# A second float32 weight group issued from ScalarE's DMA queue instead of SyncE's

## The chip, the cores and the metric

One core of a Trainium2 chip. The metric is the device time of the kernel in microseconds (us); the median of several runs is given.

## The reference

```python
batch, dim_i, dim_j, dim_k = 32, 256, 256, 128      # all inputs float32

def reference(x, y, weight):
    return np.einsum('bi,bj,kij->bk', x, y, weight).astype(np.float32)
```

The weights are 128 x 256 x 256 x 4 bytes = 33.6 MB. x, y and the output are 32, 32 and 16 KB. So this is a kernel that streams weights.

## The kernel before

The weights are cut into 32 groups of 1.05 MB. In a group each of 128 partitions holds one row of 8 KB. The kernel multiplies in bf16, and there are two ways to get there:

- 30 groups are loaded by GpSimd's DMA queue, which casts on the way ("casting loads" below). They are 11 copies, taken in order.
- Groups 0 and 16 (`FIRST`) are loaded as float32 by SyncE's queue into `w_f`, and ScalarE casts them into `w_sb`. They exist because GpSimd's loads take some microseconds to start moving data (the first casting packet starts at 5.59 us here).

```python
LOADS = (
    ((8, 24), 0, 8),
    ((4, 12, 20, 28), 0, 8),
    (tuple(range(2, 32, 4)), 0, 8),
    # ... cut: eight more, down to eighths of the last group
)
FIRST = (0, 16)

    # ... cut: shapes, buffers, semaphores
    sw = [ nc.gpsimd.dma_start(out=w_of(groups)[...], in_=rows_of(groups)[...]).then_inc(s, 16).ins
           for (groups, lo, hi), s in zip(LOADS, s_w) ]                    # shortened
    hw = [
        nc.scalar.dma_start(out=x_sb, in_=x).then_inc(s_x, 16).ins,
    ]
    for n, g in enumerate(FIRST):
        hw.append(
            nc.sync.dma_start(
                out=w_f[:, n:n + 1, :], in_=rows_of((g,)),
            ).then_inc(s_f[n], 16).ins
        )
    # ... cut: these issues are moved to the very head of the program, before the start barrier

    for n, g in enumerate(FIRST):
        for h in range(2):
            lo, hi = h * IC * J // 2, (h + 1) * IC * J // 2
            c = act.copy(out=w_sb[:, place_of[g], lo:hi], in_=w_f[:, n, lo:hi])
            if h == 0:
                c._wait_ge(s_f[n], 16)
            c.then_inc(s_act, 1)

    # ... cut: VectorE prepares xblk and y4
    pe.wait_ge(s_act, 2 * len(FIRST))
    pe.wait_ge(s_dve, t_x)
    # ... cut: TensorE multiplies unit by unit, waiting for each load; the first unit of
    #     16 groups holds groups 0 and 16 and needs the first three casting loads too
```

## Time and profile before

| | before |
|---|---|
| median of 3 runs | 84.71 us |
| span in the profile | 83.4 us |
| DMA engines working | about 1.2 to 80.8 us |
| first matmul | 41.93 us |
| TensorE / VectorE / ScalarE busy | 39% / 30% / 6% of the span |

A profile's slices tell when an engine works, but a busy engine is not yet the bound. What counts is which wait ends last: here TensorE, between its last units, stands and waits for weights. The prediction below shows those lines. To them belong the DMA queues of the kernel before (queue and kind, packets, MB, share of the 16 engines' span): q1 is SyncE's, q10 is ScalarE's.

```profile
q1 hardware_dynamic: 432, 2.11, 6.8%
q10 hardware_dynamic: 48, 0.03, 0.1%
```

SyncE's queue carries both float32 groups, ScalarE's only x. The page counts both queues' packets as a share of the same 16 DMA engines, and the trace has 16 completion entries (packets of 4 bytes) for each copy of either: 48 for SyncE's three copies, the output among them, and 16 for x.

Where a text below counts single packets ("started at", "packets of 8 KB"), the numbers come from the packet records of the trace. A copy of one float32 group is 128 packets of 8 KB, 8 for each DMA engine. A casting packet writes 4 KB of bf16 (3712 such packets in the trace), for which 8 KB of float32 are read. The records don't say which engine ran a packet, so "for each engine" is a count divided by 16, and a "round" is 16 packets.

### The profile page before, as it was taken

To read this page: it belongs to the slowest core of one execution; us is meant where nothing else is said; L and a number is where in the kernel's file an instruction comes from. 1 tells how busy PE (TensorE), PEld (TensorE's weight loads), DVE (VectorE), ACT (ScalarE), POOL (GpSimd) and SP (SyncE) were. 2 spreads that over 40 slices of the span, in tenths; PEclk is the share of its full clock that TensorE was granted. 3 is DMA by queue.
4 is the path that set the end of the run, shared out by engine and by line. 5 is a ranking of instruction groups with operands and counts; after the bars stand their busy time and mean duration, and the time that the engine had idled before them with its cause. 6 is when DMAs were issued, how large, how long until landed. Compare 5 with 4: busy or idle time off the path is not lost.

```text
span 83.4 us, 257 instructions
## 1 busy us (share of the span) xinstructions
PE 32.6 (39%) x136; PEld 4.3 (5%) x43; DVE 25.1 (30%) x28; ACT 5.2 (6%) x5; POOL 8.8 (11%) x18
## 2 busy tenths in 40 slices
PE   0000000000000000000089999996019999984780
PEld 0000000000000000000000000000000100112330
DVE  0009450000292000000000000003999900999932
ACT  0019930000000000000000000000000000000000
POOL 5999600000000000000000000000000000000000
PEclk9999999999999999999999999999995699999999
DMA  4999999999999999999999999999999999999980
GB/s 126 373 377 301 218 208 216 216 214 216 218 218 210 218 216 210 216 218 212 216 216 210 216 218 212 216 216 210 218 216 212 216 216 210 216 218 210 200 115 8
DMA packets 4912, 17.91 MB, mean 215 GB/s; under 512 B 384, under 2 KB 800, under 8 KB 4656
## 3 DMA queue, kind: packets, MB, share of 16 engines
q0 software_dynamic: 4432, 15.76, 94.3%
q1 hardware_dynamic: 432, 2.11, 6.8%
q10 hardware_dynamic: 48, 0.03, 0.1%
HBM read 33.62 MB, written 0.02 MB: 403 GB/s over the span
## 4 chain that ended last, share of the span: by engine, by line
DMA 46%; PE 39%; DVE 6%; POOL 3%; another core or an unknown queue 3%; issue 2%; POOLq 0%
DMA w_sb<-in_weight_dram 46%; PE ps L237 39%; DVE tmp L294 5%; POOL w_sb L120 2%; POOL y_sb L127 1%; DVE tmp L302 1%; POOL const-float32-0.0 L332 0%; POOLq L332 0%; POOL const-uint8-127 L332 0%; POOL const-float32-1.0 L332 0%; DVE acc L302 0%
## 5 line engine op out<-in xcount | busy, mean ns | idle before, releaser
L237 PE MATMUL ps<-w_sb,xblk 128*128 128x512 bf16 (+1 forms) x136 | 32.6, 397 | 48.9 <-DMA w_sb<-in_weight_dram 44.2
L294 DVE TENSOR_TENSOR tmp<-ps,y 128x4096 f32<-128x4096 f32 (+3 forms) x4 | 8.6, 2156 | 36.7 <-PE ps L237 36.7
L298 DVE TENSOR_REDUCE acc<-tmp 128x16 f32<-128x4096 f32 (+3 forms) x4 | 8.6, 2155 | 0.1
L237 PEld LDWEIGHTS ps<-w_sb,xblk 128*128 128x128 bf16 x43 | 4.3, 101 | 77.0 <-DMA w_sb<-in_weight_dram 42.7
L120 POOL DMA_DIRECT2D w_sb<-in_weight_dram x11 | 7.6, 702 | 0.6 <-issue 0.6
L178 ACT CAST w_sb<-w_f 128x1024 bf16<-128x1024 f32 x4 | 3.9, 1041 | 0.0
L219 DVE STREAM_TRANSPOSE yt<-y_sb 32x256 f32<-32x256 f32 x1 | 0.4, 433 | 11.0 <-DMA y_sb<-in_y_dram 11.0
L192 DVE COPY x_rep<-x_sb 32x1024 f32<-32x1024 f32 x1 | 0.8, 786 | 6.1 <-PEq L332 6.1
L198 DVE STREAM_TRANSPOSE xt<-x_rep 32x256 f32<-32x256 f32 x4 | 1.7, 435 | 0.1
L227 DVE STREAM_TRANSPOSE y<-y_rep 32x256 f32<-32x256 f32 x4 | 1.7, 435 | 0.1
L178 ACT ACT_TABLE_LOAD x1 | 1.3, 1283 | 6.0 <-PEq L332 6.0
L210 DVE TENSOR_SCALAR xblk<-xt,mask 128x256 bf16<-128x256 f32 x4 | 1.4, 498 | 0.0
L302 DVE CUSTOM_DVE_ANT_0 tmp<-ps,y 128x256 f32<-128x256 f32 x2 | 0.8, 425 | 1.6 <-PE ps L237 1.6
L222 DVE COPY y_rep<-yt 32x1024 f32<-32x1024 f32 x1 | 0.7, 683 | 0.0
L205 DVE TENSOR_REDUCE mask<-ident 128x4 f32<-128x128 f32 x1 | 0.4, 382 | 1.0 <-POOL ident L169 1.0
L127 POOL DMA_DIRECT2D y_sb<-in_y_dram x1 | 0.5, 534 | 0.0
L169 POOL TENSOR_SCALAR_AFFINE_SELECT ident<-ident 128x128 f32<-128x128 f32 x1 | 0.3, 287 | 0.1
L168 POOL MEMSET ident<- 128x128 f32 x1 | 0.3, 289 | 0.0
L302 DVE DVE_READ_ACCUMULATOR2_ANT acc<- 128x1 f32 x2 | 0.2, 84 | 0.0
L332 POOL MEMSET const-float32-0.0<- 128x1 f32 x1 | 0.1, 98 | 0.2 <-issue 0.2
L332 POOL MEMSET const-bfloat16-1.0<- 128x1 bf16 x1 | 0.1, 101 | 0.0
L332 POOL MEMSET const-uint8-127<- 128x1 uint8 x1 | 0.1, 101 | 0.0
(1 smaller groups left out, 0.1 us busy)
## 6 DMA issues: line engine op xcount, KB each, us to landing
w_sb<-in_weight_dram POOLq DMA_DIRECT2D x2, 4096.0 KB, 48.0
w_sb<-in_weight_dram POOLq DMA_DIRECT2D x2, 2048.0 KB, 43.3
w_f<-in_weight_dram SPq DMA_DIRECT2D x2, 1024.0 KB, 6.6
w_sb<-in_weight_dram POOLq DMA_DIRECT2D x2, 1024.0 KB, 40.9
w_sb<-in_weight_dram POOLq DMA_DIRECT2D x1, 512.0 KB, 72.2
w_sb<-in_weight_dram POOLq DMA_DIRECT2D x1, 256.0 KB, 72.8
w_sb<-in_weight_dram POOLq DMA_DIRECT2D x1, 128.0 KB, 72.9
w_sb<-in_weight_dram POOLq DMA_DIRECT2D x2, 64.0 KB, 72.7
```

The lines of the kernel that those rows point to most:

```text
L120: nc.gpsimd.dma_start(out=w_of(groups)[:, :, lo * J:hi * J], in_=rows_of(groups)[:, :, lo * J:hi * J],).then_inc(s, 16).ins
L127: sw.insert(2, nc.gpsimd.dma_start(out=y_sb, in_=y).then_inc(s_y, 16).ins)
L178: c = act.copy(out=w_sb[:, place_of[g], lo:hi], in_=w_f[:, n, lo:hi])
L192: t = done(v.tensor_copy(out=x_rep, in_=x_sb.rearrange("b (ip ic) -> b ic ip", ic=IC).unsqueeze(3) .to_broadcast([B, IC, IP, KK]),)._wait_ ...
L198: c = v.transpose(out=xt[q * 32:(q + 1) * 32, :, :], in_=x_rep[:, :, q * IP // Q:(q + 1) * IP // Q, :],)
L210: c = v.tensor_scalar(out=xblk[:, :, :, kk], in0=xt, scalar1=mask[:, kk:kk + 1], scalar2=None, op0=mult,)
L222: t = done(v.tensor_copy(out=y_rep, in_=yt.unsqueeze(3).to_broadcast([B, J // 32, B, KK]),)._wait_ge(s_dve, t))
L227: c = v.transpose(out=y4[q * 32:(q + 1) * 32, :].rearrange("p (jb j) -> p jb j", j=32), in_=y_rep[:, :, q * BQ:(q + 1) * BQ, :],)
L237: return pe.add_instruction(mybir.InstMatmult(name=nc.get_next_instruction_name(), engine=mybir.EngineType.PE, ins=[pe.lower_ap(rhs), pe.l ...
L294: t = done(v.tensor_tensor(out=prod, in0=sums, in1=y4.unsqueeze(1).to_broadcast([P, n_g, J]), op=mult,)._wait_ge(s_pe, n_pe))
L298: done(v.tensor_reduce(out=acc[:, unit[0]:unit[-1] + 1:unit[1] - unit[0]], in_=prod, axis=AX, op=add,)._wait_ge(s_dve, t))
L302: done(v.tensor_tensor_reduce(out=prod[:, 0, :], in0=sums[:, 0, :], in1=y4, scale=1.0, scalar=0.0, op0=mult, op1=add, accum_out=acc[:, uni ...
```

## The change

The intent: SyncE's second issue waits behind its first (0.61 us each). ScalarE has only issued x by then, so it can issue the second group at the same time, on a queue of its own.

```diff
-    for n, g in enumerate(FIRST):
+    for n, (g, queue) in enumerate(zip(FIRST, (nc.sync, nc.scalar))):
         hw.append(
-            nc.sync.dma_start(
+            queue.dma_start(
                 out=w_f[:, n:n + 1, :], in_=rows_of((g,)),
             ).then_inc(s_f[n], 16).ins
         )
```

## The prediction

Where "row" isn't a row of weights or of a profile, in the prediction and in the texts below, it means the DMA queue of an issuing engine.

> **What bounds the kernel now.** I read the page first. Its slices show where work is missing, its chain shows which work the end waits for.
>
> The slices (40 of 2.085 us; mean busy tenths of the 16 DMA engines, then GB/s counted as written), and the chain's shares of the span:
>
> ```profile
> DMA  4999999999999999999999999999999999999980
> GB/s 126 373 377 301 218 208 216 216 214 216 218 218 210 218 216 210 216 218 212 216 216 210 216 218 212 216 216 210 218 216 212 216 216 210 216 218 210 200 115 8
> ...
> DMA 46%; PE 39%; DVE 6%; POOL 3%; another core or an unknown queue 3%; issue 2%; POOLq 0%
> ```
>
> The DMA engines are full from the second slice to the second last. The chain gives PE 39% and so looks split, but it follows PE only because matmuls happen to be running; the chain in order of time shows that PE is fed group by group and goes back to waiting for weights.
>
> ```profile
> 3.17 38.71 DMA w_sb<-in_weight_dram
> ...
> 76.16 1.89 PE ps L237 x8
> 78.04 0.49 another core or an unknown queue
> 78.53 0.04 issue
> 78.57 1.03 PE ps L237 x8
> ```
>
> After each of the late units (here 1.89 us of matmuls) there is idle time that an arriving transfer ends; the page's group of the matmuls names it (48.9 us idle, 44.2 of it for weights). So the end is set by the last weight bytes, plus a tail of 2 to 3 us. The metric is some 84.7 us, of which the DMA stream takes about 1.2 to 80.8.
>
> What the stream carries, in stretches (columns: stretch, length, busy us of the five engines, clock, DMA share, GB/s written):
>
> ```profile
> 1.00:1.25 0.25, 0.00 (x0) 0.00 (x0) 0.00 (x0) 0.00 (x0) 0.20 (x1) 1.00 0.20 57
> 1.25:1.50 0.25, 0.00 (x0) 0.00 (x0) 0.00 (x0) 0.00 (x0) 0.25 (x1) 1.00 1.14 369
> 1.50:2.00 0.50, 0.00 (x0) 0.00 (x0) 0.00 (x0) 0.00 (x0) 0.50 (x2) 1.00 0.91 246
> 2.00:2.50 0.50, 0.00 (x0) 0.00 (x0) 0.00 (x0) 0.00 (x0) 0.50 (x1) 1.00 0.93 262
> 2.50:5.50 3.00, 0.00 (x0) 0.00 (x0) 0.00 (x0) 0.00 (x0) 3.00 (x5) 1.00 1.02 410
> 5.50:6.50 1.00, 0.00 (x0) 0.00 (x0) 0.42 (x1) 0.46 (x1) 1.00 (x3) 1.00 1.01 315
> 6.50:8.00 1.50, 0.00 (x0) 0.00 (x0) 1.40 (x4) 1.49 (x2) 1.50 (x3) 1.00 1.05 319
> 8.00:12.00 4.00, 0.00 (x0) 0.00 (x0) 2.45 (x7) 3.22 (x4) 1.64 (x5) 1.00 1.06 213
> 12.00:70.00 58.00, 23.49 (x93) 1.62 (x15) 11.70 (x8) 0.00 (x0) 0.00 (x0) 0.97 1.06 215
> ```
>
> A GpSimd-issued weight load reads 4 bytes for each 2 that it writes, so 215 GB/s written is 430 read. A float32 copy writes what it reads: 410 is 410. The two kinds thus differ in this column, and it tells which is running: up to 5.5 us only float32; from 5.5 to 8.0 a mixture (half of 410 and half of 213 would be 311; seen 315 and 319); after 8.0 the casting loads alone. Between 2.5 and 70 us the reading rate is 410 to 430, with no gap. Only 1.25 to 2.5 us is short of it.
>
> [...]
>
> **The change part by part.** Issues and their use, in the timeline, and the landings of the two groups, in the view of their tile:
>
> ```profile
> 0.00 1.26 SPq L134 DMA_DIRECT2D w_f<-in_weight_dram  x2
> 0.12 0.41 ACTq L130 DMA_DIRECT2D x_sb<-in_x_dram  x1
> ...
> 6.04 1.28 ACT L178 ACT_TABLE_LOAD   x1 [6.04 <-PEq L332]
> ...
> 7.33 3.88 ACT L178 CAST w_sb<-w_f 128x1024 bf16<-128x1024 f32 x4
> ```
>
> ```profile
> L134 SPq DMA_DIRECT2D w_f<-in_weight_dram x2: 586/606/627, 0.0 to 0.7; - x2
> ...
> DMA to landing us min/median/max: 4.9/6.6/8.2
> ```
>
> 1. Issue. SyncE loses one issue of about 0.61 us and ScalarE gains it. Second group now: starts about 0.65, ends 1.26. After: behind x, 0.12 + 0.41 + 0.61 = 1.14. That is 0.12 us earlier, and it is saved on no path, since the first group keeps the DMA engines in work well past that. SyncE next has the output at 82 us. ScalarE waits for a start signal until 6.04 us, so its extra 0.61 us lies in 5.5 us of idle time. Cost 0.
> 2. Bytes. The same 2 x 1.05 MB of float32, the same 31.5 MB read by casting loads, the same 16 engines. Change 0.
> 3. Landings. Up to 5.5 us the stretches sum to 14 + 92 + 123 + 131 + 1230 = 1590 KB, of which 33 are x, so 1.56 of 2.10 MB of float32 are through. Now these are the whole first group and half of the second. Afterwards the second group's first bytes should come some 0.8 us after its issue ended, as the first group's do (issue over at 0.6, first bytes about 1.4): 1.95 us. Until then the first has a lead of some 0.16 MB; then they alternate. At 5.5 us: 0.86 and 0.70 MB. With three rows active each reads a third of 430, 143 GB/s: first group through after (1.05 - 0.86)/0.143 = 1.3 us, at 6.8; the second then has 0.16 MB left at 215, through at 7.6. Landing follows the last bytes by about 0.65 us (8.2 to 8.9 now). So I expect **7.5 and 8.2 us from the span's start, against 4.9 and 8.9 now**.
> 4. Casts. The first starts at 7.33 now, when the table is loaded; it would start near 7.5. Casts end near 11.4 instead of 11.21. The first matmul is at 41.93, held by the third casting load. Slack 30 us; cost 0.
> 5. Casting loads. They give up a sixth of the rate from 5.5 to 6.8 us and have the engines alone from 7.6 instead of about 8.2. This cancels, as bytes are the same.
> 6. Start-up. Short of 430 GB/s are 1.25 to 2.5 us by 538 - 346 = 192 KB and 2.5 to 5.5 us by 60 KB: together 0.59 us at 430 GB/s, all that better feeding could win. The second row has data only from about 1.95, so it can fill 0.55 x (430 - 262) = 92 KB and the 60 KB: 152 KB, 0.35 us. The profile doesn't tell whether the shortage belongs to one row (then gained) or to the first reads whatever the row (then not). I give it somewhat less than half: 0.15 us.
>
> Sum: 84.71 - 0.15 = 84.56, rounded to 84.6.
>
> **The rivals.**
> - *The second row ends the slow start.* For it: DMA share 0.91 to 0.93 there against 1.05 later, at 60% of the rate, so packets are open but slow. Against: the slow time is nearly over when the second row gets data. It makes 84.3.
> - *Interleaved groups disturb each other in HBM* (the 4 MiB pitch). [...] Against: the casting loads of groups 8 and 24 (also 4 MiB apart) and the mixture at 5.5 to 8.0 run at full rate[...]. [...] I hold it for improbable[...].
> - *ScalarE becomes late* and with it the casts. Its slack of 30 us speaks against it; it makes no change.
> - *The casting loads start later*, because three rows share instead of two, or *earlier*. Only work-conserving reshuffling while the DMA row stays full; 84.7.
>
> **Range and chances.** Before's runs spread 84.64 to 84.9. The full start-up gain gives 84.36, none 84.71, slight disturbance 84.9; with the spread: 84.25 to 84.95. To be over 2% faster takes 1.7 us, almost three times all the shortage there is: 0.01. To be over 2% slower takes the HBM rival at full size: 0.02. Within 2%: 0.97.
>
> **What would show it.** Right: slices full of DMA as before; landings near 7.5 and 8.2; the mixture ends near 7.6 and its written rate is higher in its first part (two thirds float32: about 350 GB/s); first matmul at 41.9 within 0.4 us, all later unit waits shifted by the same amount. The start-up term is read in the stretches 1.5 to 5.5 us: 262 and 410 higher is the gain. Wrong: a float32 stretch under 380 GB/s (HBM rival), a first matmul that waits for the casts, a casting rate off 215, or a last landing moved otherwise than the first unit's.

## The result

| | before | after |
|---|---|---|
| median (6 runs each) | 84.72 us | 84.72 us |
| range | 84.63 to 84.90 | 84.63 to 84.87 |
| first matmul | 41.93 us | 41.87 us |
| last weights landed | 81.13 us | 81.07 us |

The ratio is 0.9998, 95% interval 0.9982 to 1.0013. A ratio here is the mean time of one kernel's runs over that of the other's in the same rounds, so it is not quite the ratio of the medians.

The slices of the kernel after (busy tenths of the DMA engines, GB/s written):

```profile
DMA  4999999999999999999999999999999999999980
GB/s 122 393 370 293 214 214 212 216 218 212 218 218 216 212 216 216 212 218 214 212 214 218 210 220 214 214 214 216 212 214 218 212 214 216 212 216 214 197 118 8
```

The DMA row is digit for digit that of before. The queues have changed as intended:

```profile
q1 hardware_dynamic: 288, 1.07, 3.5%
q10 hardware_dynamic: 192, 1.08, 3.3%
```

So has the timeline:

```profile
0.00 0.63 SPq L134 DMA_DIRECT2D w_f<-in_weight_dram  x1
0.12 0.42 ACTq L130 DMA_DIRECT2D x_sb<-in_x_dram  x1
...
0.58 0.56 ACTq L134 DMA_DIRECT2D w_f<-in_weight_dram  x1
...
7.33 3.88 ACT L178 CAST w_sb<-w_f 128x1024 bf16<-128x1024 f32 x4
```

ScalarE issues the second group at 0.58 us and is through at 1.14 us. Its casts start at 7.33 us as before. But the landings, counted from the issue, are these:

```profile
DMA to landing us min/median/max: 4.9/6.6/8.3
```

From the span's start that is 4.92 us for the first group and 8.83 us for the second (0.58 + 8.3, rounded). They were 4.91 and 8.89 us before. The group on its own queue gained nothing. The packet records say why. The second group's packets start at 4.19 us, when 127 of the first group's 128 have started. In the kernel before, on one queue, the first group's completion entries come at 4.21 us, so its second group's turn came at the same moment.

The stretches (columns as in the prediction's table of stretches; the last is GB/s written) answer to those of before:

```profile
1.25:1.50 0.25, 0.00 (x0) 0.00 (x0) 0.00 (x0) 0.00 (x0) 0.25 (x1) 1.00 1.35 328
1.50:2.00 0.50, 0.00 (x0) 0.00 (x0) 0.00 (x0) 0.00 (x0) 0.50 (x2) 1.00 0.70 199
2.00:2.50 0.50, 0.00 (x0) 0.00 (x0) 0.00 (x0) 0.00 (x0) 0.50 (x1) 1.00 0.95 393
2.50:5.50 3.00, 0.00 (x0) 0.00 (x0) 0.00 (x0) 0.00 (x0) 3.00 (x5) 1.00 1.02 403
5.50:6.50 1.00, 0.00 (x0) 0.00 (x0) 0.42 (x1) 0.46 (x1) 1.00 (x3) 1.00 1.03 315
6.50:8.00 1.50, 0.00 (x0) 0.00 (x0) 1.40 (x4) 1.49 (x2) 1.50 (x3) 1.00 1.03 309
```

From 1.25 to 2.5 us they sum to 82 + 99.5 + 196.5 = 378 KB, against 346 KB before. From 2.5 to 5.5 us they are 1209 KB against 1230. The two nearly cancel, and by 8 us both kernels have written 2.38 MB. Afterwards 213 and then 215 GB/s are written, as before.

### The profile page after: what moved, and what is told of

Read it like the earlier page. It is cut to its first block, busy times and chain, and to the rows that moved or that the text cites. A ratio compares the mean times of both kernels' runs of the same rounds, so it can differ in the third digit from the quotient of the medians.

```text
span 83.4 us, 257 instructions
## 1 busy us (share of the span) xinstructions
PE 32.5 (39%) x136; PEld 4.3 (5%) x43; DVE 25.2 (30%) x28; ACT 5.2 (6%) x5; POOL 8.8 (11%) x18
## 2 busy tenths in 40 slices
DMA packets 4912, 17.91 MB, mean 215 GB/s; under 512 B 384, under 2 KB 800, under 8 KB 4656
## 4 chain that ended last, share of the span: by engine, by line
DMA 46%; PE 39%; DVE 6%; POOL 3%; another core or an unknown queue 3%; issue 2%; POOLq 0%
DMA w_sb<-in_weight_dram 46%; PE ps L237 39%; DVE tmp L294 5%; POOL w_sb L120 2%; POOL y_sb L127 1%; DVE tmp L302 1%; POOL const-float32-0.0 L332 0%; POOLq L332 0%; POOL const-uint8-127 L332 0%; POOL const-float32-1.0 L332 0%; DVE acc L302 0%
```

## The experiments

The missing interleave of the two groups was the surprise. Three theories of it were held against each other: copies are served **in order** of issue; ScalarE's row was merely **behind x** and slow to come up; or an engine takes **turns**, but with some limit. A second question was what sets the time at all. Intervals below are 95%. The edits are shown against the changed kernel; times and ratios are against the kernel before, run in the same rounds. That serves for both kernels, whose times differ by 0.02%.

### The order of x and the second group

```diff
-    hw = [ nc.scalar.dma_start(out=x_sb, in_=x)... ]
+    hw = []
     # the loop over FIRST as in the changed kernel
+    hw.append(nc.scalar.dma_start(out=x_sb, in_=x).then_inc(s_x, 16).ins)
```

> ScalarE issues the second group first (about 0.12 us) and x behind it, so both float32 copies are issued at nearly the same moment and neither is behind x. Theory IN ORDER (SyncE's and ScalarE's copies are carried out one after the other, in the order of issue, whatever row they are on): the second group's packets still begin only when the first group's end, near 4.2 us; groups land near 4.9 and 8.8 us as in the changed kernel, and x lands last, near 9 us. Theory BEHIND X (ScalarE's row was merely slow to come up, or held by x before it; two rows with work do alternate): the second group's packets begin near 1.5 us, the groups land within 1 us of each other, 7.3 to 8.5 us. Both: the time stays, 84.7 within 0.2 us, since x and the casts have 30 us to spare.

Measured: 85.02 us against 84.66, ratio 1.0028 (0.9998 to 1.0057), a little outside the 0.2 us expected and not clear of no change. The second group was issued at 0.12 us, ahead of x. Its first packet started at 4.05 us, after 112 of the first group's packets, 7 for each engine. BEHIND X is refuted. IN ORDER is nearly met, but not quite: the first group's last 16 packets ran only after 16 of the second, so an engine's eighth, if the packets are spread evenly, comes after one of the second group. So turns are taken, only late. x landed at 10.3 us, which VectorE had time for.

### Three float32 groups, the third issued early or late

```diff
-FIRST = (0, 16)
+FIRST = (0, 16, 8)                 # and group 8 taken out of LOADS
-zip(FIRST, (nc.sync, nc.scalar))
+zip(FIRST, (nc.sync, nc.sync, nc.scalar))
```

The late version also issues x as three copies, of 64, 64 and 128 columns, ahead of group 8.

> A third float32 group (group 8, taken out of the first casting load): SyncE issues groups 0 and 16 at 0 and 0.65 us, ScalarE issues x and then group 8 at about 0.58 us. IN ORDER: order of service 0, 8, 16; group 8 lands near 8.8 us, group 16 near 13.5 us (the third has half of 430 GB/s beside the casting loads: 1.05 MB / 0.215 = 4.9 us). ROW BY ROW (an engine takes a whole copy of one row, then one of the other row): the same order, 0, 8, 16. ALTERNATE (packet by packet): 8 and 16 land within 1 us of each other, at 12.5 to 13.5 us. To be read together with the run that issues group 8 later. Time as before, 84.7 within 0.3 us: same bytes.

> As the run with three float32 groups, but x goes in three copies, so that ScalarE issues group 8 only at about 1.4 us, after SyncE has issued both of its groups (0 and 0.65 to 1.26 us). IN ORDER: order 0, 16, 8; group 16 lands near 8.8 us and group 8 near 13.5 us: the order of the other run is turned round by 0.8 us of issue time. ROW BY ROW: 0, 8, 16 as in the other run. ALTERNATE: 8 and 16 land within 1 us of each other. Time as before, 84.7 within 0.3 us.

Measured, early: 84.86 us, ratio 1.0022 (0.9996 to 1.0049). Issues and landings (queue, copies, KB, median us from issue to landing):

```profile
w_f<-in_weight_dram SPq DMA_DIRECT2D x2, 1024.0 KB, 8.4
w_f<-in_weight_dram ACTq DMA_DIRECT2D x1, 1024.0 KB, 11.0
```

Late: 85.05 us, ratio 1.0045 (1.0021 to 1.0070), 0.05 us outside what was expected:

```profile
w_f<-in_weight_dram SPq DMA_DIRECT2D x2, 1024.0 KB, 7.6
...
w_f<-in_weight_dram ACTq DMA_DIRECT2D x1, 1024.0 KB, 11.4
```

Early: group 0 landed at 4.9 us, group 8 at 11.5 and group 16 at 12.5. Group 8's packets started after 127 of group 0's, and from 4.90 us on the two queues' packets alternate. The landings are less than 1 us apart but earlier than I had reckoned for that. Late: group 8, issued at 1.52 us, had its first packets at 5.95 us, after 193 of SyncE's (12.1 for each engine). Group 16 landed at 10.8 us and group 8 at 13.0, in the order of issue but 2.1 us apart, more than ALTERNATE said. No theory meets all of it: IN ORDER said 8.8 and 13.5 for both runs, ROW BY ROW said group 8 before 16. What the early run shows is that packets of two queues do alternate while both have some in line; what remains is when a copy gets into the line.

### A copy twice as long ahead of it

```diff
+    nc.sync.dma_start(out=w_f[:, :2, :], in_=rows_of(FIRST[:2])).then_inc(s_f[0], 16)
+    nc.scalar.dma_start(out=w_f[:, 2:, :], in_=rows_of(FIRST[2:])).then_inc(s_f[2], 16)
```

Three float32 groups as above; groups 0 and 16 are one copy, 16 packets for each engine. The casts of both wait for it.

> Groups 0 and 16 go in ONE copy of 2.1 MB on SyncE's queue (16 packets of 8 KB for each DMA engine), a third float32 group (8) on ScalarE's behind x at 0.58 us. Theory LOOK-AHEAD (each DMA engine lines up some 8 packets ahead of the data, and takes turns between rows only when it adds to that line; seen from the last runs, where a copy issued 0.1 to 0.6 us after a first one waits for 7 to 8 of its packets and no more, and later ones do alternate): group 8's packets begin near 4.2 us, when some 8 of the 16 are through, and alternate with the rest. Rival WHOLE COPY (a copy that runs is finished first, then turns): they begin near 6.6 us, after all 16, or after 5.3 us beside casting loads only. The copy also reads the two groups in alternation, 4 MiB apart in HBM: if that pitch hurt, its rate between 2.5 and 4 us would be well under 400 GB/s.

Measured: 84.89 us against 84.88, ratio 1.0010 (0.9983 to 1.0037). ScalarE's packets started at 4.98 us, after 155 of 256 of SyncE's, or 9.7 for each engine. WHOLE COPY (all 16) is refuted. LOOK-AHEAD holds in kind, with some 10 instead of 8. After that, the records show one round of SyncE's packets, one of ScalarE's and one of casting packets in turn. The same run reads groups 0 and 16 in alternation:

```profile
2.50:3.50 1.00, 0.00 (x0) 0.00 (x0) 0.00 (x0) 0.00 (x0) 1.00 (x2) 1.00 1.01 410
3.50:4.50 1.00, 0.00 (x0) 0.00 (x0) 0.00 (x0) 0.00 (x0) 1.00 (x2) 1.00 1.17 442
```

That is 410 and 442 GB/s with the two groups 4 MiB apart in HBM. The HBM rival of the prediction does not occur in this pattern with rows of 8 KB.

### Shorter rows

```diff
+    half = IC * J // 2
+    for h, queue in enumerate((nc.sync, nc.scalar)):
+        queue.dma_start(out=w_f[:, :, h * half:(h + 1) * half],
+                        in_=rows_of(FIRST)[:, :, h * half:(h + 1) * half]).then_inc(s_f[h], 16)
```

> The same two groups as two copies of 1.05 MB in rows of 4 KB instead of 8: SyncE issues the first half rows of both groups, ScalarE the second half rows behind x (0.58 us). Each copy is 16 packets of 4 KB for an engine. Theory LOOK-AHEAD BY COUNT (some 8 packets are lined up, whatever their size): ScalarE's packets begin when 9 to 11 of SyncE's 16 are through, near 3.1 us, and then alternate; the two copies land at most 1.5 us apart. LOOK-AHEAD BY BYTES (64 KB) or WHOLE COPY: they begin near 4.2 us, when all 16 are through, as in the changed kernel; landings near 4.9 and 8.8 us. Time 84.7 within 0.4 us in all.

Measured: 87.74 us against 84.89, ratio 1.0326 (1.0283 to 1.0369): a miss on the time by 2.5 us. ScalarE's packets started at 5.74 us, after 217 of 256 of SyncE's, 13.6 for each engine. That lies between both theories, so the unit of the look-ahead stays open. The loss is in these stretches:

```profile
2.50:3.50 1.00, 0.00 (x0) 0.00 (x0) 0.00 (x0) 0.00 (x0) 1.00 (x3) 1.00 0.68 172
3.50:4.50 1.00, 0.00 (x0) 0.00 (x0) 0.00 (x0) 0.00 (x0) 1.00 (x2) 1.00 0.84 197
```

172 and 197 GB/s, where copies with rows of 8 KB move about 400 (410 in the kernel before and 403 in the changed one, from 2.5 to 5.5 us). The DMA share is 0.68 and 0.84, so the engines were partly without packets. What held them up was not found.

### The second group issued after the start signal

```diff
-    for n, (g, queue) in enumerate(zip(FIRST, (nc.sync, nc.scalar))):   # only group 0 here
+    act.dma_start(out=w_f[:, 1:2, :], in_=rows_of(FIRST[1:])).then_inc(s_f[1], 16)
     for n, g in enumerate(FIRST):                                       # the casts
```

> The second float32 group is issued by ScalarE only after its start signal at 6.04 us. The first group's packets end near 4.5 us and the casting loads' packets begin near 5.5 us. If the end follows from how long the DMA engines are without work (my theory), about 1.0 us of emptiness between them is added to the time: 85.5 to 85.9 us. Rival: the casting loads begin late because the float32 copies hold the engines; then they begin near 4.5 us here, nothing is empty and the time stays at 84.7. Rival two: ScalarE's later casts (landing of the group near 12 us, casts to 14 us) matter; they have 28 us to spare, so no.

Measured: 86.02 us against 84.66, ratio 1.0147 (1.0098 to 1.0196); the runs are 85.31, 86.13, 85.90 and 86.31. The GB/s of the slices of the profiled run:

```profile
GB/s 90 402 181 216 250 312 318 218 215 215 215 215 218 218 216 213 213 211 216 215 215 218 218 215 213 213 213 215 216 215 218 216 213 211 213 215 217 199 104 8
```

The third slice (4.2 to 6.3 us) has 181 GB/s, nearer to the 213 of casting loads alone than to the 410 of float32 (both in the kernel before): their first packet started at 4.52 us, where the first group's ended. So the casting loads are ready by then and in the kernels before and after (first casting packet at 5.59 and 5.48 us) stand behind float32 packets. That half of the rival was right, and my hole of 1 us was not there. Still the time rose; that it lies near the forecast is luck. The profiled run was the fastest of the four (+0.6 us). In it the reading of the stretch from 4.5 to 6.0 us is 356 GB/s (178 written, twice), not 430, and by 5.5 us it is behind the kernel before by 0.19 MB, which is 0.44 us of reading at 430. The 0.6 to 1.0 us more of the other three runs has no profile and stays open.

### More work for ScalarE

```diff
+    for n in range(16):                     # into a buffer of its own, after the first group landed
+        c = act.copy(out=busy[:, n % 8, :], in_=w_f[:, 0, :IC * J // 2])
+        # waits and s_act counts cut; TensorE waits for 16 more of s_act
```

> The changed kernel with 16 more casts of 1.04 us each on ScalarE ahead of the four that matter, so these end near 28 us instead of 11.2. My theory (the casts have 30 us to spare, the first matmul waits for a casting load that lands at 41.8 us): time 84.7 within 0.2 us. Rival (ScalarE's order of work reaches the end through the casts): up to 16 us more, 100 us.

Measured: 84.91 us against 84.88, ratio 1.0016 (0.9992 to 1.0040). Its timeline:

```profile
7.33 15.24 ACT L177 CAST busy<-w_f 128x1024 bf16<-128x1024 f32 x16
...
22.48 3.88 ACT L186 CAST w_sb<-w_f 128x1024 bf16<-128x1024 f32 x4
...
42.05 3.17 PE L245 MATMUL ps<-w_sb,xblk 128*128 128x512 bf16 x7 [42.05 <-DMA w_sb<-in_weight_dram]
```

The casts that matter start at 22.48 instead of 7.33 us, and the first matmul still waits for a weight load. ScalarE is off the path.

### Both groups on ScalarE's queue

```diff
-zip(FIRST, (nc.sync, nc.scalar))
+zip(FIRST, (nc.scalar, nc.scalar))
```

> Both float32 groups on ScalarE's queue behind x, none on SyncE's: the first group is issued at 0.55 to 1.15 us instead of 0 to 0.6, so that its first packets come near 1.95 us instead of 1.41. Theory START (what the DMA engines lack at the start is carried to the end one for one): 0.4 to 0.6 us more, 85.1 to 85.3 us, less what a quicker ramp after 1.95 us gives back. Rival (the casting loads fill in, or the slow first microsecond is over at 2.5 us whoever runs): 84.7 us.

Measured: 85.38 us against 84.88, ratio 1.0068 (1.0050 to 1.0085), which is 0.6 us. The stretches:

```profile
2.00:2.50 0.50, 0.00 (x0) 0.00 (x0) 0.00 (x0) 0.00 (x0) 0.50 (x1) 1.00 0.85 279
2.50:3.50 1.00, 0.00 (x0) 0.00 (x0) 0.00 (x0) 0.00 (x0) 1.00 (x3) 1.00 0.92 319
3.50:4.50 1.00, 0.00 (x0) 0.00 (x0) 0.00 (x0) 0.00 (x0) 1.00 (x2) 1.00 0.98 410
```

The first packets start at 2.00 us, 0.58 us later than in the changed kernel, and the slow start is there again, 279 and 319 GB/s up to 3.5 us. It moves with the first copy, not with the time since the program's start. START holds: the first packets are 0.59 us later than in the kernel before (1.41 us), the last landing 0.57 us (81.70 against 81.13 us).

### Half a group less, in two ways (wrong results on purpose)

```diff
 # half rows of 4 KB:                    # half the partitions, rows of 8 KB:
+ out=w_f[:, n:n + 1, :hi]              + out=w_f[:hi * KK, n:n + 1, :]
+ in_=rows_of((g,))[:, :, :hi]          + in_=rows_of((g,))[:hi]
 # the casts of what is missing read the half that was loaded (half rows) or group 0's data
```

> A result that is wrong on purpose: only half of the second float32 group is loaded (0.52 MB less), and its second half is cast from the first group's. All instructions on the engines stay. Theory BYTES (the end is set by the bytes through 16 full DMA engines): 0.52 MB / 430 GB/s = 1.2 us less, 83.5 us within 0.2. Rival (a float32 group beside the casting loads is free, or the chain of matmuls sets the end): 84.7 us.

> Wrong on purpose, as the run with half a group, which took the half away by halving each row to 4 KB and won 0.6 us instead of 1.2. Here the second group keeps rows of 8 KB and loses half of its partitions (4 packets of 8 KB for each DMA engine instead of 8). Theory BYTES, with rows of 4 KB on these queues being slow by themselves (in the half-group run the float32 stretch from 4.5 to 5.5 us moved 262 GB/s against 397): now the full 1.2 us, 83.5 us within 0.25. Rival (a float32 group is worth only 0.6 us for its half, since the casting loads don't come sooner than 5.5 us and the engines stand empty before): 84.1 us, with a gap in the DMA row before 5.5 us.

Measured: 84.22 us against 84.88, ratio 0.9929 (0.9913 to 0.9946), and 84.22 us against 84.89, ratio 0.9916 (0.9882 to 0.9949). Both win 0.6 to 0.7 us and not 1.2, so BYTES was wrong in its size in both. The second run's rival said 84.1 us, which is close, but its sign, a gap in the DMA row before 5.5 us, isn't there (share 1.17 and 0.95 from 3.5 to 5.5 us). For the run with half rows, the stretches before and during the halved copy:

```profile
3.50:4.50 1.00, 0.00 (x0) 0.00 (x0) 0.00 (x0) 0.00 (x0) 1.00 (x2) 1.00 1.04 401
4.50:5.50 1.00, 0.00 (x0) 0.00 (x0) 0.00 (x0) 0.00 (x0) 1.00 (x2) 1.00 1.07 262
```

The rate falls from 401 to 262 GB/s at full DMA share as soon as the 4 KB rows run. In the run with 64 partitions the copy's later packets took about 600 ns instead of 320. By the packet records the halved copies kept an engine busy for 2.1 and 1.9 us on average, the whole one for 2.6, where half would be 1.3. So half the bytes saved 0.5 to 0.7 us of the engines' time, and that is about what the kernel won. In these two runs the gain follows the engines' time, not the bytes. As a test of BYTES by its size the two runs are not clean.

### Two attempts to start sooner

```diff
+    for lo, hi in ((0, 8), (8, IP)):            # second attempt: ((0, IP // 2), (IP // 2, IP))
+        nc.sync.dma_start(out=w_f[lo * KK:hi * KK, :1, :],
+                          in_=rows_of(FIRST[:1])[lo:hi]).then_inc(s_f[0], 16)
     # the cast of group 0 waits for 32
```

> An attempt to be faster than both: SyncE's first copy is a quarter of group 0 (32 partitions), its second the other 96, since x (32 partitions, issued at 0.12 us) has its first packets 1.03 us after its issue and the 128-partition copy 1.41 us. Theory START (DMA work lost at the start is carried to the end): first weight packets near 1.1 us instead of 1.4, 0.1 to 0.3 us less, 84.4 to 84.6 us. Rival (the second copy's issue, or a start that is slow whoever comes first, takes it back): 84.7 us, or up to 0.2 us more.

> The attempt to start sooner, mended: the run with a quarter first spread its copies over fewer DMA engines (20 completion packets for two copies in the trace, where 32 are usual), and waited for those that had most. Here the first group goes as two copies of 64 partitions, which divide evenly over 16 engines. First packets came 1.03 us after issue for x with 32 rows, 1.41 for 128 rows, so near 1.2 us here. Theory START: 0.1 to 0.2 us less, 84.6 to 84.7 against about 84.8 of the kernel before in these sessions; 36 completion packets' worth of engines all used evenly. Rival (the ramp to 2.5 us is the same whoever comes first): 84.8, no difference over 0.1 us.

Measured: 89.08 us against 84.89, ratio 1.0478 (1.0449 to 1.0507), and 85.86 us, ratio 1.0104 (1.0078 to 1.0129). Both are slower than either kernel, and no run found a version that beats both.

The quarter first: the trace has 20 completion entries for its two copies, where two copies of 128 partitions have 32. If an entry stands for an engine, as 16 for a whole copy suggests, at least one of them ran on fewer than 16 engines. The completions were uneven: those of the third casting load lie between 41.72 and 46.30 us, a spread of 4.6 us, where the kernel before has 0.5. The last of them decides: the first matmul starts at 46.34 us.

The halves: they have 32 completion entries for the two copies, as many as two whole copies have (and not the 36 of the expectation), and lose otherwise.

```profile
2.00:2.50 0.50, 0.00 (x0) 0.00 (x0) 0.00 (x0) 0.00 (x0) 0.50 (x1) 1.00 1.34 410
2.50:3.50 1.00, 0.00 (x0) 0.00 (x0) 0.00 (x0) 0.00 (x0) 1.00 (x3) 1.00 1.06 229
3.50:4.50 1.00, 0.00 (x0) 0.00 (x0) 0.00 (x0) 0.00 (x0) 1.00 (x2) 1.00 0.79 221
```

From 2.5 to 4.5 us 229 and 221 GB/s flow, about half of the 410 in the kernel before, and most packets up to 3.9 us take about 600 ns. Why was not found. It does not follow the 64 partitions alone: most first packets in the run with 64 partitions took 320 to 350 ns and the second round of the first half here 309 to 350, and the second group's first ones, on all partitions, took 600 as well. The first weight packet came at 1.45 us, not at 1.2: a smaller copy didn't start sooner.

This run also tells how the two queues line up. SyncE issued the first half at 0 us, ScalarE its group at 0.54, SyncE the second half at 0.71. The packets ran as 64 of the first half, then 96 of ScalarE's, then the first 16 of the second half (from 5.72 us), and in turns only after that. So here the copy that waited was on the queue that was first: it stood behind 10 rounds, 4 of its own queue and 6 of the other's. The early run with three groups shows the same: group 16, issued at 0.68 us behind group 8 at 0.58, first ran at 4.90 us, behind 128 packets of its own queue and 31 of the other. In both runs the order of issue set the line, whichever queue a copy was on.

### Where each loss or gain is made

Landings of the third casting load (which releases the first matmul) and of the last weights, in us, and their distance from the kernel before. Each row is one profiled execution; that of "x last" was the slowest of its four and that of "issue after the start signal" the fastest, so small distances are partly those of single executions.

| run | third load | last load | third, from before | last, from before |
|---|---|---|---|---|
| before | 41.89 | 81.13 | | |
| after | 41.83 | 81.07 | -0.06 | -0.06 |
| x last | 42.34 | 81.59 | +0.45 | +0.46 |
| issue after the start signal | 42.47 | 81.71 | +0.58 | +0.58 |
| both on ScalarE | 42.46 | 81.70 | +0.58 | +0.58 |
| half group, half rows | 41.37 | 80.62 | -0.52 | -0.51 |
| half group, 64 partitions | 41.36 | 80.61 | -0.53 | -0.52 |
| rows of 4 KB | 44.91 | 84.15 | +3.02 | +3.02 |
| quarter first | 46.30 | 85.54 | +4.41 | +4.41 |
| halves first | 43.02 | 82.26 | +1.13 | +1.13 |

Every distance is complete before the first matmul and is carried to the end unchanged: 39.24 us pass between the two landings in all of them, within 0.02 us. The landing of the first casting load (12.51 us in the kernel before) already has the whole distance in seven of the nine rows, as +3.02 us with rows of 4 KB and +4.41 with a quarter first; "x last" has +0.21 by then, and with the issue after the start signal the copies come in another order. From 15 to 40 us every one of these runs reads 10.76 to 10.80 MB. Not all of a distance is lost bytes: with rows of 4 KB 0.92 MB less has been read by 10 us, which is 2.1 us at 430 GB/s, and the rest is unevenness, as the third load's 16 completions lie between 43.06 and 44.91 us (before: 41.40 to 41.89). This is the firmest finding, and it says what the change could have bought: only something that the DMA engines do in these first microseconds.

## Why the prediction was right, and where it was not

The time was right (84.6 with 84.25 to 84.95; measured 84.72), and so was "no change": a transfer was moved to another queue in front of DMA engines that were full before and after (the DMA row is the same, digit for digit). Two errors had no effect on the time or its range: the landings, off by up to 2.6 us, had 30 us of slack behind them, and the gain of 0.15 us that was forecast (measured 0.0, interval -0.15 to +0.11 us) was too small to leave the range. Point by point:

1. **Issue: right.** ScalarE was through with it at 1.14 us, as reckoned, 0.12 us sooner, and it cost nothing.
2. **Bytes: right.** 4912 packets and 17.91 MB in both profiles. That lost or won DMA work is what moves the end is shown by the table above; the runs with fewer bytes agree in direction only.
3. **Landings: wrong.** The step that failed is "Until then the first has a lead of some 0.16 MB; then they alternate", with first bytes of the second group at 1.95 us. They came at 4.19 us, and the groups landed at 4.92 and 8.83 us instead of 7.5 and 8.2. Turns are taken, as the runs with three groups show, but a later copy first waits for what is lined up: 7.0 rounds of 8 KB packets when it was issued at 0.12 us, 9.7 at 0.55, 9.9 and 10 at 0.68 and 0.71 (three groups early, halves first) and 12.1 at 1.52. One group has 8 rounds, so the second queue, issued at 0.58 us, behaved like the first. That packets are lined up ahead in the order of issue fits these runs (the quarter-first run, with 20 completion entries instead of 32, can't be compared); which unit does it, and whether it counts packets, bytes or time, is open.
4. **Casts: right.** They started at 7.33 us; with 15 us more of work ahead of them the time did not change.
5. **Casting loads: right in the sum, wrong in the detail.** 315 and 309 GB/s from 5.5 to 8.0 us, the even mixture of before, instead of 350 in its first part; that followed from point 3.
6. **Start-up: wrong by its 0.15 us.** The second queue could not fill the slow stretch, since it had no turn before 4.19 us. And the run with both groups on ScalarE shows the slow stretch again behind a later first copy, so it goes with the first reads, whatever the queue. (The 84.3 of the rival on the start should read 84.4: 84.71 - 0.35 = 84.36.)

The HBM rival was refuted for this pattern (410 and 442 GB/s), as was ScalarE's lateness. Of the rivals on the start, "not then" was the right one.

## What to carry to other kernels

With the DMA engines full from the first microseconds to the last, moving a transfer to another issuing queue, issued about when it was before, changed here neither its place in the line (first packets of the second group at 4.2 us in both) nor the end (84.72 us both); look first whether the engines ever lack work. What they lost here in their first microseconds was carried to the end one for one, so see that the first copies are early, in long rows and not split. In the landing of the last weights a start 0.6 us later cost 0.6 us here, rows of 4 KB instead of 8 cost 3.0, a split into a quarter and the rest 4.4, and one into halves 1.1. Before trusting that two queues interleave, read both landings: the copy issued 0.58 us behind another waited here for nearly all of that copy of 1 MB (127 of 128 packets).
